# A decoder block: the head's transfers and casts in another order, and four background steps moved from Down to Up

## The chip, the cores and the metric

The kernel runs on one core of a Trainium2 chip. The metric is the device time of one execution in microseconds. A core has the engines TensorE (PE in the profile, with its weight loads as PEld), VectorE (DVE), ScalarE (ACT), GpSimd (POOL) and SyncE (SP); a DMA is issued by an instruction on the queue of one of them (here nearly always SP) and carried out by 16 DMA engines.

## The reference

One layer of a pre-norm decoder block in float32, 2048 tokens of width 1024:

```python
h = rmsnorm(x, norm_mix_g)
u = einsum('bsd,dc->bsc', h, w_in)                  # 1024 x 3584
gate_b, gate_c, v, x_r, g = split(u, ...)
y_conv = gate_b * causal_dwconv(gate_c * v, conv_w)
xr     = causal_dwconv(x_r, rnn_conv_w) + rnn_conv_b
y_rnn  = rg_lru(xr, w_a, b_a, w_x, b_x, lam) * gelu(g)
y = concat([rmsnorm(y_conv, g_norm_conv), rmsnorm(y_rnn, g_norm_rnn)])
x = x + einsum('bsc,cd->bsd', y, w_out)             # 1536 x 1024
z = square(relu(einsum('bsd,df->bsf', rmsnorm(x, norm_mlp_g), w_mlp_in)))   # 1024 x 4096
x = x + einsum('bsf,fd->bsd', z, w_mlp_out)         # 4096 x 1024
out = rmsnorm(x, final_norm_g)
```

`rg_lru` is a gated linear recurrence along the sequence: two block-diagonal projections, sigmoids, an exponential and a scan.

## The kernel before

**Numbers.** Every float32 operand of a matmul is split into a high part (a cast to fp32r, on ACT) and a low part (the difference, on VectorE); a product is the sum of three matmul passes: high by high, low by high and high by low. `split_into` (L179 to 181) does the split for weights. So a weight tile goes through DMA ("raw" or "w"), ACT ("w_hi") and DVE ("w_lo") before TensorE can use all of it.

**Stages.** The tokens are cut into four blocks of 512. Blocks 0 and 1 run through plain mixers (input projection by columns, conv, recurrence, output projection by rows, named "po"), blocks 2 and 3 through paired ones. The MLP takes two blocks at a time and has two halves, Up (w_mlp_in, "up", L854) and Down (w_mlp_out, "dn", L972), both with the seven products of a Strassen-Winograd scheme, in the order 1, 2, 6, 5, 7, 3, 4. Up walks 8 column slices of 7 products; Down 4 slices (s = 0 to 3) of 7 products of two halves (i is the product, a the half), some 5.44 us each. n counts products (Up) or halves (Down). `BG_FROM` (L40), the loop over Up and the loop over Down (around L2203) decide at which n a background step is taken.

**Background work.** The paired mixers need sums of weight tiles. They are made ahead of time by a generator: `prepare_sums` (63 steps) and `prepare_out_sums` (21 steps, L1283 to 1320; tiles w_out and t, three groups of seven steps). A step has up to two VectorE rows, a cast on ACT and DMAs to and from DRAM. `step()` is called in the mixer of block 1 (18 calls), in Up (30 calls) and in Down (37 calls) of the first MLP pair.

**The head.** Before the first product, x (transposed, in quarters "xT", two transfers of 256 KB each) and the first column unit of w_in (in quarters "raw", 256 KB) are loaded (L354 to 365). Quarters 0 and 1 of w are issued on ACT's queue, 2 and 3 on SP's, behind their xT. TensorE meanwhile runs warm-up matmuls on ones (L485, L487). For each quarter ACT scales xT to h_hi (L494) and casts w_hi (L498), VectorE makes h_lo (L499) and w_lo (L508), and TensorE runs 12 matmuls "start_x" (L515). After four quarters follows the next unit, "start_g" (L239). A small activation on `warm` (L369 to 370) loads the table of Sqrt ahead of time. In `lru_take`, the last three columns of the token block before ("halo") are copied into the first columns of xr_in, on ACT (L632); the new halo is saved on GpSimd (L637).

**What sets the order.** The program is written engine-agnostic in source order and laid out by a scheduling framework, which keeps the source order of an engine only in regions marked for manual scheduling. These are: the head (ACT, DVE and PE), the pair before the MLP (PE, ACT and DVE) and the MLP (PE). The mixers of blocks 0 and 1 are laid out by the scheduler, ACT and DVE of the MLP as well.

Of the kernel before, what the change touches and what calls it, by code (L numbers as in the profile page):

```python
# [9 lines left out]
F32 = mybir.dt.float32  # L10
F32R = mybir.dt.float32r
AF = mybir.ActivationFunctionType
ALU = mybir.AluOpType
MUL, ADD, SUB, MAX = ALU.mult, ALU.add, ALU.subtract, ALU.max

P = 128
# [20 lines left out]
IN_AHEAD = 3  # L37
SOONER = 200
PERIOD = 4
BG_FROM = 14  # L40
BG_UNITS = 24
BG_STEPS = 2
ORDER = (1, 2, 6, 5, 7, 3, 4)
# [21 lines left out]
def block_kernel(  # L65
# [15 lines left out]
    nc = tc.nc  # L81
    V = nc.vector
# [7 lines left out]
    cp = ctx.enter_context(tc.tile_pool(name="cp", bufs=1))  # L90
# [15 lines left out]
    def temp(name, shape=(P, 2, TB), dt=F32):  # L106
        if name in elsewhere:
            return wp.tile(list(shape), dt, tag="w", name=name)
        return tp.tile(list(shape), dt, tag="t", name=name)

    def wtile(name, shape, dt=F32):
        return wp.tile(list(shape), dt, tag="w", name=name)
# [25 lines left out]
    units = []  # L138
# [11 lines left out]
    raws = {}  # L150
# [125 lines left out]
    make_identity(nc, ident)  # L276
    ones_raw = temp("ones_raw", (P, P))
    nc.gpsimd.memset(ones_raw, 1.0)
    ones_r = cp.tile([P, P], F32R, name="ones_r")
    nc.scalar.copy(ones_r, ones_raw)  # L280
    ones = ones_r.bitcast(F32)
# [65 lines left out]
    def start_w(u, i):  # L347
        srcs, shape = units[u][1]
        raws.setdefault(u, []).extend(load_tiles(srcs[i : i + 1], shape, "raw", wtile))
# [2 lines left out]
    prm = cp.tile([P, nrows], F32, name="prm")  # L352
    nc.sync.dma_start(prm, rows_t)
    for q in range(4):  # L354
        r = temp("xT")
        for i in range(2):
            k0 = 256 * q + 128 * i
            nc.sync.dma_start(r[:, i, :], x_t[k0 : k0 + P, 0:TB])
        xtt[0, q] = r
        if q % 2 == 0:  # L360
            raws.setdefault(0, []).append(wtile("raw", units[0][1][1]))
        ks = slice(2 * (q % 2), 2 * (q % 2) + 2)
        (nc.scalar if q < 2 else nc.sync).dma_start(
            raws[0][q // 2][:, ks, :], units[0][1][0][q // 2][:, ks, :]
        )
    start_w(1, 0)
    start_w(1, 1)
    load_x(0)
    warm = cp.tile([P, 1], F32, name="warm")  # L369
    nc.scalar.activation(warm, ones_raw[:, 0:1], AF.Sqrt)  # L370
    off = {}
    o = 0
    for nm, n in ROWS:
# [86 lines left out]
    def new_h():  # L460
        return (
            hp.tile([P, KD, TB], F32R, tag="h", name="h_hi"),
            hp.tile([P, KD, TB], F32R, tag="h", name="h_lo"),
        )
# [15 lines left out]
    with tc.manual_schedule(  # L480
        engines={nc.scalar.engine, nc.vector.engine, nc.tensor.engine}
    ):
        h = new_h()
        for _ in range(WARM):
            nc.tensor.matmul(start_x[:, 0, :P], ones_raw, ones_raw, start=True, stop=True)  # L485
        for _ in range(WARM):
            nc.tensor.matmul(start_x[:, 0, :P], ones_raw, ones_raw, start=True, stop=True)  # L487
        his = [wtile("w_hi", units[0][1][1], F32R) for _ in range(2)]
        los = [wtile("w_lo", units[0][1][1], F32R) for _ in range(2)]
        w = (his, los)  # L490
        for q in range(4):
            n, ks = q // 2, slice(2 * (q % 2), 2 * (q % 2) + 2)
            for k in (2 * q, 2 * q + 1):
                nc.scalar.activation(  # L494
                    h[0][:, k], xtt[0, q][:, k % 2], AF.Copy, scale=gmix[:, k : k + 1]
                )
                if k % 2 == 0:
                    nc.scalar.copy(his[n][:, ks], raws[0][n][:, ks])  # L498
                V.scalar_tensor_tensor(  # L499
                    h[1][:, k],  # L500
                    xtt[0, q][:, k % 2],
                    gmix[:, k : k + 1],
                    h[0][:, k].bitcast(F32),
                    MUL,
                    SUB,
                )
                if k % 2 == 0:
                    V.tensor_tensor(  # L508
                        los[n][:, ks], raws[0][n][:, ks], his[n][:, ks].bitcast(F32), SUB
                    )  # L510
        for q in range(4):
            for n, (a, c) in enumerate(((0, 0), (0, 1), (1, 0))):
                for k in (2 * q, 2 * q + 1):
                    for j in range(2):
                        nc.tensor.matmul(  # L515
                            start_x[:, j],
                            w[a][k // 4][:, k % 4, j * P : (j + 1) * P],
                            h[c][:, k],
                            start=k == 0 and n == 0,
                            stop=k == KD - 1 and n == 2,  # L520
                        )
        raws.pop(0)
        cursor[0] = 1
        split_unit(1)
        w = take("g0", ahead=0)
        load_unit(2)
        s2 = squares(0, range(NT))
        split_unit(2)
        diag = diagonal(norm_rows(s2, NT), NT)
        start_g = psum("start_g")  # L530
        mm_cols(start_g, w, h, 0, ks=range(4))
        mm_cols(start_g, w, h, 1, ks=range(4))
        mm_cols(start_g, w, h, 0, ks=range(4, KD))
        mm_cols(start_g, w, h, 1, ks=range(4, KD))
        w = take("x1", ahead=0)
        start_x1 = psum("start_x1")
        mm_cols(start_x1, w, h, 0, ks=range(4))
        mm_cols(start_x1, w, h, 1, ks=range(4))
        bc = spread(diag, NT)
        mm_cols(start_x1, w, h, 0, ks=range(4, KD))  # L540
        mm_cols(start_x1, w, h, 1, ks=range(4, KD))
        nc.scalar.copy(row0[:, 0], bc)
        nc.scalar.activation(row0[:, 1], bc, AF.Square)
# [39 lines left out]
    halo = cp.tile([P, NLRU, 3], F32, name="halo")  # L583
# [45 lines left out]
    def lru_take(pr, psx, row=None):  # L629
        c0 = 2 * pr  # L630
        xr_in = wide("xr_in", 3)
        nc.scalar.copy(xr_in[:, :, 0:3], halo[:, c0 : c0 + 2, :])  # L632
        if row is None:
            nc.scalar.copy(xr_in[:, :, 3:], psx)
        else:
            V.tensor_mul(xr_in[:, :, 3:], psx, row)
        nc.gpsimd.tensor_copy(halo[:, c0 : c0 + 2, :], xr_in[:, :, TB : TB + 3])  # L637
        return xr_in
# [1189 lines left out]
    def pair_before_mlp(b, ups):  # L1828
# [172 lines left out]
        xs = {}  # L2001
        ss = {}
        gm = cp.tile([P, KD], F32, name="gm")
        nc.sync.dma_start(gm, mlp_g_t)

        def square(b, t, i, first):
            if first:
# [105 lines left out]
    def mlp(b, ups, r0, r1, t2, rest, xs, turns_at, prepared):  # L2113
# [6 lines left out]
        for n in range(-LEAD1, len(seq)):  # L2120
# [12 lines left out]
            s, i = seq[n]  # L2133
# [11 lines left out]
            later_operands(n, r0, r1, t2)  # L2145
            if b < PAIRED and BG_FROM <= n < len(seq) - 6 and i != 3:
                step()
# [22 lines left out]
        more = b + 2 < NB  # L2170
        seq = [(s, i, a) for s in range(NS // 2) for i in ORDER for a in range(2)]
        fetched = 5
        for n in range(-LEAD2, len(seq)):
            m = n + LEAD2
            if m < len(seq):
                s, i, a = seq[m]
# [12 lines left out]
            while fetched < min(n + LEAD2 + 3, len(seq)):  # L2189
                s, i, a = seq[fetched]  # L2190
                downs[s].fetch(i, a, Z)
                fetched += 1
            s, i, a = seq[n]
# [6 lines left out]
                downs[s].multiply_last(ends[1].tiles(ends[0]))  # L2200
            if i == 7 and s + 1 < NS // 2:
                downs[s + 1].load(a)
            if more and n > 6 and (s < 2 or s == 2 and i != 4 or i in (1, 2)):  # L2203
                step()
            if more and s == NS // 2 - 1:
                if (i, a) == (6, 1):
# [2 lines left out]
                if i in (7, 3):  # L2209
                    q = 2 * (i == 3) + a  # L2210
# [123 lines left out]
```

## Time and profile before

| what | value |
|---|---|
| median of 3 runs (lowest to highest) | 2114.38 us (2113.29 to 2116.30) |
| the profiled execution | 2114.52 us |
| its span, first to last instruction | 2112.7 us |
| mean granted TensorE clock | 0.998 |
| busy ScalarE / VectorE | 52% / 76% |

The profile shows one execution. Its page gives the busy time of the engines, the costliest groups of instructions and the chain that ended last; the trace behind it gives a timeline (start, duration, engine, line, operation, output <- inputs, and in brackets the idle time before it with what ended it), waits by engine, and tables by stretch of time. The chain that ended last is TensorE for 85% of the span:

```profile
PE 85%; DVE 4%; issue 1%; DMA 1%; ACT 1%; SPq 0%; DVEq 0%; ACTq 0%
DMA  9988889743576779778765656776343455854432
```

The second row is the busy share of the DMA engines in 40 slices of 52.8 us; the first six slices, up to 317 us, have 8 or 9 tenths.

### The profile page before, as it was taken

Reading aid. Unit: us, or ns where it says so; the run is one execution under the profiler, and the core shown is the slowest. Engines: PE = TensorE matmul, PEld = TensorE weight load, DVE = VectorE, ACT = ScalarE, POOL = GpSimd, SP = SyncE. Lnnn points to the kernel's source line nnn. Section 1 sums busy time; section 2 is a strip of 40 time slices with the busy share of each in tenths; the row PEclk is TensorE's granted clock in tenths of the full one; section 3 lists DMA queues with packets and bytes.
Section 4 is the critical chain, followed back from the end, with each engine's and each line's share of the span. In section 5 each row is a group of like instructions: output and inputs, shape, how many; then the busy total and the mean of one; then the engine's idle time right before and its main releaser. Section 6 shows DMA issues by size and latency. Waiting matters only on the chain.

```text
span 2112.7 us, 25180 instructions
## 1 busy us (share of the span) xinstructions
PE 2098.0 (99%) x9396; PEld 1727.0 (82%) x9396; DVE 1603.8 (76%) x1857; ACT 1106.0 (52%) x1448; POOL 52.2 (2%) x62
## 2 busy tenths in 40 slices
PE   9999999999999999999999999999999999999998
PEld 7888888888888888888788887888888888888886
DVE  6889637858766688998997876785886765887776
ACT  6885357626554554444456888234764333333344
POOL 0000001000000000000100100000000000000000
PEclk9999999999999999999999999999999999999999
DMA  9988889743576779778765656776343455854432
GB/s 323 331 313 321 316 333 338 296 170 114 186 269 250 278 265 336 271 268 303 288 228 206 223 210 220 271 264 212 120 164 135 149 180 209 306 182 149 140 120 80
DMA packets 204875, 492.99 MB, mean 233 GB/s; under 512 B 15952, under 2 KB 80464, under 8 KB 204752
## 3 DMA queue, kind: packets, MB, share of 16 engines
q1 hardware_dynamic: 202768, 486.13, 64.0%
q10 hardware_dynamic: 1984, 5.24, 0.6%
q8 instruction: 74, 1.21, 0.2%
q14 instruction: 49, 0.40, 0.1%
HBM read 324.59 MB, written 166.72 MB: 233 GB/s over the span
## 4 chain that ended last, share of the span: by engine, by line
PE 85%; DVE 4%; issue 1%; DMA 1%; ACT 1%; SPq 0%; DVEq 0%; ACTq 0%
PE up L854 40%; PE dn L972 26%; PE po L266 5%; PE wo_x L1798 3%; PE ps_g L239 2%; PE ps_x L239 2%; PE wo_w L1798 2%; PE ps_c L239 1%; PE ps_v L239 1%; PE wo_y L1798 1%; PE tps L1652 1%; PE dn L991 1%; PE psri L1411 1%; PE ps_b L239 1%; DVE u L759 0%
## 5 line engine op out<-in xcount | busy, mean ns | idle before, releaser
L854 PE MATMUL up<-H,w_hi 128*128 128x512 f32 x2576 | 794.9, 390 | 0.0
L854 PEld LDWEIGHTS up<-H,w_hi 128*128 128x128 f32 x2576 | 482.4, 188 | 102.6 <-issue 1.8
L854 PE MATMUL up<-H,w_lo 128*128 128x512 f32 x1288 | 501.4, 389 | 0.0
L972 PE MATMUL dn<-w_lo,z_hi 128*128 128x512 f32 x864 | 336.5, 389 | 1.2 <-DVE w_lo L181 1.2
L972 PE MATMUL dn<-w_hi,z_lo 128*128 128x512 f32 x864 | 336.1, 389 | 0.0
L972 PE MATMUL dn<-w_hi,z_hi 128*128 128x512 f32 x864 | 336.1, 389 | 0.0
L854 PEld LDWEIGHTS up<-H,w_lo 128*128 128x128 f32 x1288 | 241.8, 188 | 51.0 <-DVE w_lo L181 0.7
L180 ACT CAST z_hi<-z 128x1024 fp32r<-128x1024 f32 x112 | 118.0, 1053 | 272.3 <-PE dn L972 214.9
L181 DVE TENSOR_TENSOR w_lo<-w,w_hi 128x1024 fp32r<-128x1024 f32 x156 | 190.2, 1221 | 75.4 <-ACT w_hi L180 27.5
L180 ACT CAST w_hi<-w 128x1024 fp32r<-128x1024 f32 x156 | 162.8, 1049 | 138.8 <-PE up L854 67.9
L972 PEld LDWEIGHTS dn<-w_lo,z_hi 128*128 128x128 f32 x864 | 162.2, 188 | 35.7 <-DVE w_lo L181 2.3
L972 PEld LDWEIGHTS dn<-w_hi,z_lo 128*128 128x128 f32 x864 | 162.2, 188 | 33.8
L972 PEld LDWEIGHTS dn<-w_hi,z_hi 128*128 128x128 f32 x864 | 162.2, 188 | 33.7
L1004 DVE TENSOR_TENSOR x<-dn,x 128x1024 f32<-128x1024 f32 x108 | 130.6, 1220 | 23.9 <-PE dn L972 23.7
L181 DVE TENSOR_TENSOR z_lo<-z,z_hi 128x1024 fp32r<-128x1024 f32 x112 | 136.5, 1218 | 5.4 <-ACT z_hi L180 5.4
L866 ACT COPY snap<-up 128x1024 f32<-128x1024 f32 x48 | 48.7, 1014 | 67.6 <-PE up L854 67.3
L871 ACT ACTIVATE snap<-snap 128x1024 f32<-128x1024 f32 x33 | 35.1, 1062 | 74.4 <-DVE snap L891 28.5
L181 DVE TENSOR_TENSOR w_lo<-raw,w_hi 128x1024 fp32r<-128x1024 f32 x44 | 53.3, 1220 | 13.2 <-ACT w_hi L180 10.7
L266 PE MATMUL po<-w_hi,y_hi 128*128 128x512 f32 x192 | 60.0, 394 | 0.4 <-DVE ys_B L623 0.4
L266 PE MATMUL po<-w_hi,y_lo 128*128 128x512 f32 x192 | 59.7, 391 | 0.3 <-DVE y_lo L596 0.3
L1798 PE MATMUL wo_x<-w_o,y_hi 128*128 128x512 f32 x192 | 59.8, 392 | 0.0
L266 PE MATMUL po<-w_lo,y_hi 128*128 128x512 f32 x192 | 59.3, 389 | 0.0
(415 smaller groups left out, 3290.3 us busy)
## 6 DMA issues: line engine op xcount, KB each, us to landing
z<-d_z SPq DMA_DIRECT2D x112, 512.0 KB, 6.2
w<-in_w_mlp_in_dram SPq DMA_DIRECT2D x64, 512.0 KB, 6.1
d_z<-snap SPq DMA_DIRECT2D x64, 512.0 KB, 3.5
w_hi<-d_w SPq DMA_DIRECT2D x55, 512.0 KB, 6.6
w_lo<-d_w SPq DMA_DIRECT2D x55, 512.0 KB, 6.2
d_z<-z SPq DMA_DIRECT2D x48, 512.0 KB, 3.4
w<-in_w_mlp_out_dram SPq DMA_DIRECT2D x48, 512.0 KB, 7.5
d_w<-w_hi SPq DMA_DIRECT2D x40, 512.0 KB, 6.2
```

Source lines behind the costliest of these rows:

```text
L180: nc.scalar.copy(hi, src)
L181: return (lo_engine or V).tensor_tensor(lo, src, hi.bitcast(F32), SUB).ins
L239: nc.tensor.matmul(ps[:, j, lo:hi], ws[k // 4][:, k % 4, j * P : (j + 1) * P], hs[:, k, lo:hi], start=k == 0 and i == 0, stop=k == KD - 1 ...
L266: nc.tensor.matmul(ps[:, half, :], ys[:, j, t * P : (t + 1) * P], ws[j][:, 0, half * 512 : (half + 1) * 512], start=first and i == 0, stop ...
L854: nc.tensor.matmul(ps[:, j, :], ws[:, k, j * P : (j + 1) * P], hs(k), start=i in (1, 2, 5) and k == 0 and n == 0, stop=k == 3 and n == len ...
L866: made_at["snap"] = nc.scalar.copy(t, ps).ins
L871: nc.scalar.activation(t, t, AF.Relu)
L972: nc.tensor.matmul(ps[t // 2][:, t % 2, :], zs[:, p, t * P : (t + 1) * P], ws[:, p, :], start=i in (1, 2, 5) and a == 0 and p == 0 and n == 0,
L991: nc.tensor.matmul(self.x[t // 2][:, t % 2, :], zs[:, p, t * P : (t + 1) * P], ws[:, p, :], start=False, stop=a == 1 and p == 1 and n == 2 ...
L1004: V.tensor_add(xt[b, th, dh], ps[th], xt[b, th, dh])
L1411: nc.tensor.matmul(ps[:, e, :], ws[own, c - gates[2], :], xsrc[own, j, :], start=i == 0, stop=i == 2,)
L1798: nc.tensor.matmul(ps[t // 2][:, t % 2, :], ys[:, j, t * P : (t + 1) * P], ws[:, j, :], start=first and n == 1, stop=final and n == 6 * le ...
```

## The change

1. `BG_FROM` goes from 14 to 10, and Down takes no background steps in s = 3 any longer (products 1 and 2, both halves). Up makes 34 calls and Down 33, so every step that comes after n = 9 is taken four calls sooner.
2. The warm Sqrt activation is issued before the cast of ones_r. Both used a table load of their own; the program now has one there.
3. In the head w's quarter 0 is issued on ACT's queue, and quarters 1 to 3 on SP's, each ahead of the xT quarter of the same number.
4. In each quarter w_hi is cast before both h_hi, and w_lo is made after both h_lo.
5. The copy of halo into xr_in goes from ACT to GpSimd, and the load of gm from SP's queue to GpSimd's.

```diff
--- before.py
+++ after.py
@@ -37,7 +37,7 @@
 IN_AHEAD = 3
 SOONER = 200
 PERIOD = 4
-BG_FROM = 14
+BG_FROM = 10
 BG_UNITS = 24
 BG_STEPS = 2
 ORDER = (1, 2, 6, 5, 7, 3, 4)
@@ -276,6 +276,8 @@
     make_identity(nc, ident)
     ones_raw = temp("ones_raw", (P, P))
     nc.gpsimd.memset(ones_raw, 1.0)
+    warm = cp.tile([P, 1], F32, name="warm")
+    nc.scalar.activation(warm, ones_raw[:, 0:1], AF.Sqrt)
     ones_r = cp.tile([P, P], F32R, name="ones_r")
     nc.scalar.copy(ones_r, ones_raw)
     ones = ones_r.bitcast(F32)
@@ -352,22 +354,20 @@
     prm = cp.tile([P, nrows], F32, name="prm")
     nc.sync.dma_start(prm, rows_t)
     for q in range(4):
+        if q % 2 == 0:
+            raws.setdefault(0, []).append(wtile("raw", units[0][1][1]))
+        ks = slice(2 * (q % 2), 2 * (q % 2) + 2)
+        (nc.sync if q else nc.scalar).dma_start(
+            raws[0][q // 2][:, ks, :], units[0][1][0][q // 2][:, ks, :]
+        )
         r = temp("xT")
         for i in range(2):
             k0 = 256 * q + 128 * i
             nc.sync.dma_start(r[:, i, :], x_t[k0 : k0 + P, 0:TB])
         xtt[0, q] = r
-        if q % 2 == 0:
-            raws.setdefault(0, []).append(wtile("raw", units[0][1][1]))
-        ks = slice(2 * (q % 2), 2 * (q % 2) + 2)
-        (nc.scalar if q < 2 else nc.sync).dma_start(
-            raws[0][q // 2][:, ks, :], units[0][1][0][q // 2][:, ks, :]
-        )
     start_w(1, 0)
     start_w(1, 1)
     load_x(0)
-    warm = cp.tile([P, 1], F32, name="warm")
-    nc.scalar.activation(warm, ones_raw[:, 0:1], AF.Sqrt)
     off = {}
     o = 0
     for nm, n in ROWS:
@@ -490,12 +490,11 @@
         w = (his, los)
         for q in range(4):
             n, ks = q // 2, slice(2 * (q % 2), 2 * (q % 2) + 2)
+            nc.scalar.copy(his[n][:, ks], raws[0][n][:, ks])
             for k in (2 * q, 2 * q + 1):
                 nc.scalar.activation(
                     h[0][:, k], xtt[0, q][:, k % 2], AF.Copy, scale=gmix[:, k : k + 1]
                 )
-                if k % 2 == 0:
-                    nc.scalar.copy(his[n][:, ks], raws[0][n][:, ks])
                 V.scalar_tensor_tensor(
                     h[1][:, k],
                     xtt[0, q][:, k % 2],
@@ -504,10 +503,9 @@
                     MUL,
                     SUB,
                 )
-                if k % 2 == 0:
-                    V.tensor_tensor(
-                        los[n][:, ks], raws[0][n][:, ks], his[n][:, ks].bitcast(F32), SUB
-                    )
+            V.tensor_tensor(
+                los[n][:, ks], raws[0][n][:, ks], his[n][:, ks].bitcast(F32), SUB
+            )
         for q in range(4):
             for n, (a, c) in enumerate(((0, 0), (0, 1), (1, 0))):
                 for k in (2 * q, 2 * q + 1):
@@ -629,7 +627,7 @@
     def lru_take(pr, psx, row=None):
         c0 = 2 * pr
         xr_in = wide("xr_in", 3)
-        nc.scalar.copy(xr_in[:, :, 0:3], halo[:, c0 : c0 + 2, :])
+        nc.gpsimd.tensor_copy(xr_in[:, :, 0:3], halo[:, c0 : c0 + 2, :])
         if row is None:
             nc.scalar.copy(xr_in[:, :, 3:], psx)
         else:
@@ -2001,7 +1999,7 @@
         xs = {}
         ss = {}
         gm = cp.tile([P, KD], F32, name="gm")
-        nc.sync.dma_start(gm, mlp_g_t)
+        nc.gpsimd.dma_start(gm, mlp_g_t)
 
         def square(b, t, i, first):
             if first:
@@ -2200,7 +2198,7 @@
                 downs[s].multiply_last(ends[1].tiles(ends[0]))
             if i == 7 and s + 1 < NS // 2:
                 downs[s + 1].load(a)
-            if more and n > 6 and (s < 2 or s == 2 and i != 4 or i in (1, 2)):
+            if more and n > 6 and (s < 2 or s == 2 and i != 4):
                 step()
             if more and s == NS // 2 - 1:
                 if (i, a) == (6, 1):
```

Lines of the changed kernel after the head are two below those of the kernel before. Since a scheduler lays out much of the program, an edit can move rows far away from it. Three places follow.

ACT from the start of the program (the head). Before:

```order
L363 DMA raw<-in_w_in_dram 128x2x256
L280 ACT_TABLE_LOAD
L280 CAST ones_r<-ones_raw 128x128
L363 DMA raw<-in_w_in_dram 128x2x256
L370 ACT_TABLE_LOAD
L370 ACTIVATE warm<-ones_raw 128x1
L494 ACTIVATE h_hi<-xT,prm 128x512
L632 COPY xr_in<-halo 128x2x3 x3
L498 CAST w_hi<-raw 128x512
L494 ACTIVATE h_hi<-xT,prm 128x512 x2
L498 CAST w_hi<-raw 128x512
```

and in the changed kernel:

```order
L360 DMA raw<-in_w_in_dram 128x2x256
L280 ACT_TABLE_LOAD
L280 ACTIVATE warm<-ones_raw 128x1
L282 CAST ones_r<-ones_raw 128x128
L493 CAST w_hi<-raw 128x512
L495 ACTIVATE h_hi<-xT,prm 128x512 x2
L493 CAST w_hi<-raw 128x512
L495 ACTIVATE h_hi<-xT,prm 128x512 x2
L493 CAST w_hi<-raw 128x512
L495 ACTIVATE h_hi<-xT,prm 128x512 x2
```

One of two table loads is gone from ahead of the first h_hi, the issue of the second quarter of w and the copies of halo are gone, and each w_hi stands in front of both h_hi of its quarter.

DVE in the output projection of block 0, in the rows that lead to the last y_lo of the recurrence (v<-r,v is the decay of the recurrence, w_lo_1389, w_lo_1472 and w_lo_1476 are low parts of coming weights, y_lo_1375 and y_lo_1462 of the projection's operand). Before:

```order
L738 TENSOR_TENSOR gc_1312<-ps_c_1263,row0_125 128x1024
L181 TENSOR_TENSOR w_lo_1389<-raw_1245,w_hi_1388 128x1024
L605 TENSOR_TENSOR v_573<-v_573,v_1142 128x1024
L700 TENSOR_TENSOR gi_1315<-gi_1315,xr_1147 128x1024
L430 TENSOR_SCALAR diag_hi_1356<-ident_81,rs_x_1034 128x128 x2
L431 SCALAR_TENSOR_TENSOR diag_lo_1357<-ident_81,rs_x_1034,diag_hi_1356 128x128 x2
L430 TENSOR_SCALAR diag_hi_1356<-ident_81,rs_x_1034 128x128 x2
L431 SCALAR_TENSOR_TENSOR diag_lo_1357<-ident_81,rs_x_1034,diag_hi_1356 128x128 x2
L181 TENSOR_TENSOR w_lo_1472<-raw_1380,w_hi_1471 128x1024
L714 SCALAR_TENSOR_TENSOR v_1339<-r_1314,v_1339 128x1024
L181 TENSOR_TENSOR w_lo_1476<-raw_1382,w_hi_1475 128x1024
L715 TENSOR_SCALAR r_1314<-v_1339 128x1024
```

and in the changed kernel:

```order
L712 SCALAR_TENSOR_TENSOR v_1339<-r_1314,v_1339 128x1024
L181 TENSOR_TENSOR w_lo_1389<-raw_1245,w_hi_1388 128x1024
L713 TENSOR_SCALAR r_1314<-v_1339 128x1024
L594 SCALAR_TENSOR_TENSOR y_lo_1375<-s_448,prm_92,y_hi_1374 128x512
L714 SCALAR_TENSOR_TENSOR v_1339<-v_1339 128x1024
L594 SCALAR_TENSOR_TENSOR y_lo_1375<-s_448,prm_92,y_hi_1374 128x512
L744 TENSOR_TENSOR cv_1449<-ps_v_1400,gc_1312 128x2x512
L755 TENSOR_SCALAR u_1453<-cv_1449,prm_92 128x512 x2
L716 TENSOR_TENSOR gi_1315<-gi_1315,v_1339 128x1024
L181 TENSOR_TENSOR w_lo_1472<-raw_1380,w_hi_1471 128x1024
L719 SCALAR_TENSOR_TENSOR v_1339<-r_1314,state_398,gi_1315 128x512
L181 TENSOR_TENSOR w_lo_1476<-raw_1382,w_hi_1475 128x1024
```

w_lo_1389 and w_lo_1472 stood ahead of v<-r,v, and stand behind it now; w_lo_1476 stood right behind it, and stands five rows later. The w_hi casts that these need moved on ACT in the same way.

DVE in the last slice of Down (s = 3). x<-dn,x adds a product of Down to its sum, L1304 to L1308 and w_out<-w_out,sum_hi are background rows, and w_lo<-w_7852 before is w_lo<-w_7871 in the changed kernel. Before:

```order
L1004 TENSOR_TENSOR x_6365<-dn,x_6365 128x1024
L181 TENSOR_TENSOR z_lo<-z,z_hi 128x1024
L181 TENSOR_TENSOR w_lo<-w_7302,w_hi 128x1024
L1304 TENSOR_TENSOR t_7948<-w_out 128x1024
L1305 TENSOR_TENSOR w_out<-w_out 128x1024
L942 TENSOR_TENSOR t_8001<-w_7858,w_7856 128x1024
L1308 TENSOR_TENSOR w_out<-w_out 128x1024
L181 TENSOR_TENSOR t_7948<-t_7948,sum_hi 128x1024
L181 TENSOR_TENSOR z_lo<-z,z_hi 128x1024
L181 TENSOR_TENSOR w_lo<-w_7852,w_hi 128x1024
```

and in the changed kernel:

```order
L181 TENSOR_TENSOR w_lo<-w_7318,w_hi 128x1024
L181 TENSOR_TENSOR w_out<-w_out,sum_hi 128x1024
L1002 TENSOR_TENSOR x_6384<-dn,x_6384 128x1024
L1002 TENSOR_TENSOR x_6386<-dn,x_6386 128x1024
L181 TENSOR_TENSOR w_out<-w_out,sum_hi 128x1024
L181 TENSOR_TENSOR z_lo<-z,z_hi 128x1024
L181 TENSOR_TENSOR w_lo<-w_7871,w_hi 128x1024
L940 TENSOR_TENSOR t_8027<-w_7877,w_7875 128x1024
L1002 TENSOR_TENSOR x_6697<-dn,x_6697 128x1024
L941 TENSOR_TENSOR w_7875<-w_7875,w_7871 128x1024
```

Between w_lo<-w_7302 (w_lo<-w_7318 now) and the next w_lo stood four background rows and a sum of weights; now there are two background rows, and the sum comes behind it.

## The prediction

> **What bounds the kernel now.** The page's first part comes first: TensorE is busy almost throughout, so a change that leaves its matmuls alone can win only what is missing from that line.
>
> ```profile
> PE 2098.0 (99%) x9396; PEld 1727.0 (82%) x9396; DVE 1603.8 (76%) x1857; ACT 1106.0 (52%) x1448; POOL 52.2 (2%) x62
> ```
>
> The span is 2112.7 us and the profiled execution's own time 2114.52, so 1.82 us lie outside the span; the median of the runs shown, 2114.38, is 0.14 below that execution. Of the span, 2112.7 - 2098.0 = 14.7 us have no matmul in them. The view of waits, cut to TensorE, says where it stood still (us in total, times, longest), and it has five rows only:
>
> ```profile
> PE start_x L515 <- ACT w_hi L498: 2.4, 1, 2.4
> PE dn L972 <- DVE w_lo L181: 1.2, 2, 0.6
> PE start_x L485 <- POOL ones_raw L278: 1.1, 1, 1.1
> PE po L266 <- DVE ys_B L623: 0.4, 1, 0.4
> PE po L266 <- DVE y_lo L596: 0.3, 1, 0.3
> ```
>
> The head, two waits in Down and the output projection of blocks 0 and 1 are the places to look at; the tail (some 9 us behind the last matmul) is not touched. Then the timeline of the head, with each row's start and duration:
>
> ```profile
> 1.23 1.28 ACT L280 ACT_TABLE_LOAD   x1 [1.23 <-PEq L2300]
> 2.82 1.28 ACT L370 ACT_TABLE_LOAD   x1
> 3.85 1.58 PE L487 MATMUL start_x<-ones_raw 128*128 128x128 f32 x12
> 6.24 0.72 ACT L494 ACTIVATE h_hi<-xT,prm 128x512 fp32r<-128x512 f32 x1 [1.92 <-DMA xT<-in_x_t_dram]
> 6.87 0.38 ACT L632 COPY xr_in<-halo 128x6 f32<-128x6 f32 x3
> 7.15 0.61 ACT L498 CAST w_hi<-raw 128x512 fp32r<-128x512 f32 x1
> 7.82 2.07 PE L515 MATMUL start_x<-h_hi,w_hi 128*128 128x512 f32 x4 [2.38 <-ACT w_hi L498]
> 12.07 1.08 PE L515 MATMUL start_x<-h_hi,w_hi 128*128 128x512 f32 x4
> 14.80 1.07 PE L515 MATMUL start_x<-h_hi,w_hi 128*128 128x512 f32 x4
> 20.24 0.39 PE L239 MATMUL start_g<-h_hi,w_hi 128*128 128x512 f32 x1
> ```
>
> The warm-up matmuls end at 3.85 + 1.58 = 5.43, and TensorE waits for the chain "xT lands, h_hi, halo copies, w_hi". From the second quarter on, a quarter of 12 matmuls takes 14.80 - 12.07 = 2.73 us, 0.227 each. The first took 12.07 - 7.82 = 4.25. The table by stage says why (PEclk is the last number but two):
>
> ```profile
> 5.00:6.00 1.00, 0.43 (x4) 0.24 (x3) 0.00 (x0) 0.00 (x0) 0.00 (x0) 1.00 1.01 338
> 6.00:7.00 1.00, 0.00 (x0) 0.00 (x0) 0.00 (x1) 0.76 (x3) 0.00 (x0) 1.00 1.00 374
> 8.00:9.00 1.00, 1.00 (x3) 0.78 (x4) 1.00 (x2) 1.00 (x3) 0.00 (x0) 0.50 1.04 333
> 11.00:12.00 1.00, 1.00 (x6) 0.83 (x5) 1.00 (x3) 1.00 (x2) 0.00 (x0) 1.00 1.02 341
> ```
>
> The granted clock was halved at 8 us and back at 11, right behind the idle stretch; so the head lost 2.4 us of waiting and some 1.5 more to the clock. The DMA share is 1.0 there: transfers land one behind the other, 262 KB at about 374 GB/s, which is 0.70 us each.
>
> **Head: what it gains.** The order of ACT's instructions in the changed kernel is: one table load (1.28 us, at 1.23), the warm activation, ones_r, then the first w_hi cast, then both h_hi. ACT is so free by about 3.1 instead of 4.3, and w_hi is out of the way as soon as w's first quarter is in; that quarter has ACT's queue to itself. After xT lands only h_hi (0.72) stands before the first matmul; in the rows above it was 7.82 - 6.24 = 1.58, so 0.86 us come from the order. The rest comes from the landing. Before, w's second quarter shared the engines from the first microseconds; now its 0.70 us of traffic stand behind xT's first two transfers. I take xT's first half at 5.5 instead of 6.2 and the first matmul at 6.25. TensorE then idles 6.25 - 5.43 = 0.8 us instead of 2.4. In the first quarter the second h_hi follows a landing 0.7 later, and w_lo now stands behind both h_lo, which together cost about 0.35 us on the path; I set 3.07 us for the quarter, and 3 x 2.73 for the other three. start_g begins at 6.25 + 3.07 + 8.19 = 17.5 instead of 20.24: **-2.8 us**, on the assumption that the clock stays full. If it is halved again for the same stretch, the first quarter costs some 1.5 us more and the gain is 1.3. The upper bound is 3.2 (no small wait in the first quarter).
>
> The lead has to be fed. start_g's third matmul needs the next unit's w_lo, and that chain is bound by a landing:
>
> ```profile
> 15.27 1.05 ACT L180 CAST w_hi<-raw 128x1024 fp32r<-128x1024 f32 x1 [0.94 <-DMA raw<-in_w_in_dram]
> 16.36 1.23 DVE L181 TENSOR_TENSOR w_lo<-raw,w_hi 128x1024 fp32r<-128x1024 f32 x1 [1.24 <-ACT w_hi L180]
> ```
>
> The bytes ahead of it are the same, so it is ready at 16.36 + 1.23 = 17.59 again, and needed at 17.5 + 0.45 = 17.95: just in time. A larger lead would not be kept. The gm transfer leaves SP's queue (it stood behind x, the warm-up's last load) and three small copies leave ACT; GpSimd is 2% busy, and its nearest row is a copy of the same kind:
>
> ```profile
> 165.59 1.11 POOL L747 COPY haloc<-cv 128x4 f32<-128x4 f32 x1 [16.32 <-DVE cv L746]
> ```
>
> A halo copy there lies beside the product whose conv it feeds (10.9 us for one of 48 matmuls), so both are at nothing, from -0.4 (the row at 6.87, if ACT were short) to +1.1 for a conv that waits once.
>
> [...]
>
> **Down: what it gains.** The two waits of 0.6 us are in the last of the four column slices (s = 3), where VectorE runs back to back and background work stands between an accumulation and the w_lo that TensorE needs next:
>
> ```profile
> 996.72 1.22 DVE L1004 TENSOR_TENSOR x<-dn,x 128x1024 f32<-128x1024 f32 x1 [1.50 <-PE dn L972]
> 1000.13 1.22 DVE L1304 TENSOR_TENSOR t<-w_out 128x1024 f32<-128x1024 f32 x1
> 1007.07 1.22 DVE L181 TENSOR_TENSOR w_lo<-w,w_hi 128x1024 fp32r<-128x1024 f32 x1
> 1007.40 0.39 PE L972 MATMUL dn<-w_hi,z_hi 128*128 128x512 f32 x1
> 1008.34 0.50 PE L972 MATMUL dn<-w_lo,z_hi 128*128 128x512 f32 x1 [0.55 <-DVE w_lo L181]
> 1030.05 0.39 PE L972 MATMUL dn<-w_hi,z_hi 128*128 128x512 f32 x1
> 1031.04 0.50 PE L972 MATMUL dn<-w_lo,z_hi 128*128 128x512 f32 x1 [0.60 <-DVE w_lo L181]
> ```
>
> Starts are 0.227 apart elsewhere, so the two cost 1008.34 - 1007.40 - 0.23 = 0.71 and 1031.04 - 1030.05 - 0.23 = 0.76. VectorE issues one such row every 1.15 us (996.72 to 1007.07 is nine steps). From the x addition to the first late w_lo there are ten rows, four of them background (two are quoted); in the changed order there are five. The second late w_lo has two background rows ahead of it, which are gone too. Five and two rows are 5.7 and 2.3 us of slack against 0.7 and 0.8 of waiting. So **-1.47 us**, bounds 0 and -1.5.
>
> The steps do not vanish: each comes four calls earlier. Four run in Up at n = 10 to 13, and the third block of out sums now lies on the turn from s = 1 to s = 2. I counted VectorE's rows there: from the addition behind n = 27 to the w_lo of n = 32 there are 17 rows of 1.15 us, 19.6 us, ready some 1.0 to 1.3 us before TensorE comes to it. No stall, but little margin, a rival. In Up, TensorE waits for nothing, and a step is at most two VectorE rows and a cast beside products of 10.9 us each; at nothing, bounds 0 and the 0.7 of one such stall.
>
> **Output projection of block 0: a loss.** Here nothing was edited, but the scheduler lays the rows out anew. On ACT three w_hi casts move from in front of the sigmoids to behind them, and the w_lo that belong to them move with them, to a place where VectorE is never idle.
>
> ```profile
> 148.41 0.69 ACT L694 ACTIVATE r<-psri,prm 64x512 f32<-64x512 f32 x1
> 161.43 1.22 DVE L714 SCALAR_TENSOR_TENSOR v<-r,v 128x1024 f32<-128x1024 f32 x1 [0.76 <-ACT r L708]
> 179.50 0.75 DVE L596 SCALAR_TENSOR_TENSOR y_lo<-s,prm,y_hi 128x512 fp32r<-128x512 f32 x1
> 180.31 0.74 PE L266 MATMUL po<-w_hi,y_lo 128*128 128x512 f32 x2 [0.30 <-DVE y_lo L596]
> ```
>
> From 161.43 to 179.50 VectorE runs without a gap, and the second half of y_lo is already 0.6 us late (0.30 shown as idle, 0.57 against the usual spacing). Counted in both orders from "v<-r,v" to that y_lo, the change has two w_lo more, 2 x 1.15 = 2.3 us; the start of the stretch stays: ahead of "r" on ACT one w_hi cast is gone (1.05), its input s comes one VectorE row sooner (1.15), and a table load (1.28) and the first sigmoid (0.69) now stand behind s instead of ahead of it, which is 0.2 us sooner in all. TensorE's own order is the same, so the stall grows from 0.6 to some 2.6: **+2.0 us**, bounds 0 (the chain starts that much earlier) and +2.5.
>
> **Output projection of block 1: a small gain.** In the new order one y_hi and one y_lo fewer stand before bcs and ys_B:
>
> ```profile
> 420.33 0.97 PEld L615 LDWEIGHTS po<-ones_r,v 128*128 128x128 f32 x8 [0.58 <-ACT bcs L1135]
> 423.03 0.73 PE L266 MATMUL po<-w_hi,y_hi 128*128 128x512 f32 x2 [0.40 <-DVE ys_B L623]
> ```
>
> The two waits cost about 0.31 and 0.56 us against the usual spacing; a y_hi half is 0.7 us on ACT, a y_lo half 0.7 on VectorE, so most of both goes: **-0.7 us**, bounds 0 and -0.87.
>
> **Sum:** 2114.52 - 2.8 + 2.0 - 0.7 - 1.47 = 2111.55 for an execution like the profiled one, and 0.14 less, 2111.4, against the median.
>
> **Rivals.**
> 1. *The re-laid order costs nothing in the output projection.* For it: the loss rests on a count of rows, and the chain of block 0 hangs on several engines, each of which could start sooner. Against it: y_lo was late already and nothing ahead of it went away. Then 2111.4 - 2.0 = 2109.4.
> 2. *The half clock stays.* For it: 0.50 was granted right after an idle stretch in which TensorE had worked before and after. Against it: only a third of the idle time is left. Or the landing does not move, as the engines carry 338 to 374 GB/s already, which costs 0.7. Either gives 2111.4 + 1.5 = 2112.9, at most.
> 3. *The stall in Down only moves.* The turn from s = 1 to s = 2 has about 1 us of margin; two more VectorE rows (2.3 us) there, and it waits 1.2 us, as s = 3 does now: 2111.4 + 1.5 = 2112.9.
> 4. *Slower.* The four early steps take tiles of the common pool while Up still holds the norm's and the sums' tiles. If one takes a tile that a load of Up's weights needs, that load is issued a product later and TensorE waits for the whole chain behind it:
>
> ```profile
> L180 ACT CAST w_hi<-w 128x1024 fp32r<-128x1024 f32 x156 | 162.8, 1049 | 138.8 <-PE up L854 67.9
> L181 DVE TENSOR_TENSOR w_lo<-w,w_hi 128x1024 fp32r<-128x1024 f32 x156 | 190.2, 1221 | 75.4 <-ACT w_hi L180 27.5
> w<-in_w_mlp_in_dram SPq DMA_DIRECT2D x64, 512.0 KB, 6.1
> ```
>
>  That is 6.1 + 1.05 + 1.22 = 8.4 us, 2111.4 + 8.4 = 2119.8. It decides from the point where the pool has no free tile at n = 12 or 13. Against it: loads go out three products ahead (33 us), and no wait of TensorE in Up is in the view above.
>
> **How the numbers follow.** Chances: the forecast 0.40, rival 1 0.30, rival 2 0.12, rival 3 0.07, rival 4 0.11. 0.2% of 2114.38 is 4.2 us, about what a measurement of this kernel can tell from no change: faster is below 2110.15, slower above 2118.6. Rival 1 is faster in nine cases of ten (0.27), the forecast in its better fifth (0.09): 0.36. Slower is nearly all of rival 4: 0.10. The rest, 0.54, is within 0.2%. The range's lower end takes every term at its better bound, 2114.4 - 3.2 - 0.87 - 1.5 = 2108.8; the upper takes the poorest head and the full loss in the projection, with the gain of Down and half of that in block 1: 2114.4 - 1.3 + 2.5 - 1.47 - 0.4 = 2113.7, with 1.2 for a stall that moves, 2114.9. Of the same, the forecast's own spread is 2110.2 to 2112.6.
>
> **What would show it.** Right: the first data matmul near 6.3 and start_g near 17.5, no clock of 0.5 between 7 and 11 us, no wait of dn for w_lo in s = 3, one wait of po for y_lo of about 2.5 us near 177, and waits of po for bcs and ys_B gone or halved. Wrong: a first quarter still at 4 us (rival 2), no long y_lo wait (rival 1), a dn wait near 950 (rival 3), a wait of up for w_hi or w_lo in the first 14 products (rival 4). A matmul count or order that differs outside the places named, or waits of several us in the first 150 us, would make the sum itself wrong.

## The result and the profile after

| | before | changed |
|---|---|---|
| median of 19 runs each (lowest to highest) | 2114.55 us (2112.84 to 2117.75) | 2117.75 us (2116.18 to 2120.26) |
| ratio, 95% interval | | 1.0016 [1.0009, 1.0023] |
| profiled execution, span | 2114.52, 2112.7 us | 2118.50, 2116.7 us |
| mean granted clock | 0.998 | 0.996 |

The change makes the kernel 3.2 us slower; the forecast was 3.0 us faster (2111.4), with 2114.9 as the upper end of its range. The view of TensorE's waits in the changed kernel (us in total, times, longest):

```profile
PE po L266 <- DVE y_lo L594: 4.9, 2, 3.6
PE start_x L485 <- POOL ones_raw L278: 1.1, 1, 1.1
PE dn L970 <- DVE w_lo L181: 0.8, 1, 0.8
PE start_x L513 <- ACT h_hi L495: 0.6, 1, 0.6
```

The head's wait fell from 2.4 to 0.6 us, Down's two waits in s = 3 and block 1's ys_B are gone. In their place stands one line that was 0.3 us before: po waiting for y_lo, now 4.9. (The dn wait of 0.8 lies in the second MLP, at 1830 us; it was 0 to 0.5 us in the executions of the experiments and is not followed here.)

The head in the changed kernel's timeline (start, duration):

```profile
4.79 0.72 ACT L495 ACTIVATE h_hi<-xT,prm 128x512 fp32r<-128x512 f32 x1 [0.29 <-DMA xT<-in_x_t_dram]
5.57 0.73 PE L513 MATMUL start_x<-h_hi,w_hi 128*128 128x512 f32 x2
6.89 0.73 PE L513 MATMUL start_x<-h_hi,w_hi 128*128 128x512 f32 x2 [0.59 <-ACT h_hi L495]
17.55 0.39 PE L239 MATMUL start_g<-h_hi,w_hi 128*128 128x512 f32 x1
```

start_g begins at 17.55 instead of 20.24, 2.7 us sooner. Then the output projection of block 0, TensorE's rows and VectorE's:

```profile
175.38 0.61 PE L266 MATMUL po<-w_lo,y_hi 128*128 128x512 f32 x2
179.59 1.22 PE L266 MATMUL po<-w_hi,y_lo 128*128 128x512 f32 x2 [3.60 <-DVE y_lo L594]
183.79 1.22 PE L266 MATMUL po<-w_hi,y_lo 128*128 128x512 f32 x2 [1.27 <-DVE y_lo L594]
...
162.51 1.23 DVE L712 SCALAR_TENSOR_TENSOR v<-r,v 128x1024 f32<-128x1024 f32 x1 [1.02 <-ACT r L706]
178.80 0.74 DVE L594 SCALAR_TENSOR_TENSOR y_lo<-s,prm,y_hi 128x512 fp32r<-128x512 f32 x1
183.00 0.74 DVE L594 SCALAR_TENSOR_TENSOR y_lo<-s,prm,y_hi 128x512 fp32r<-128x512 f32 x1
```

Both halves of y_lo are late. The second one starts 3.5 us later than before (183.00 against 179.50), for a TensorE that is 2.7 us earlier. And the pair of matmuls behind each wait takes 1.22 us, where it took 0.74 before (the row at 180.31), because of the clock (last number but two):

```profile
178.00:180.00 2.00, 0.41 (x1) 0.41 (x2) 2.00 (x4) 1.31 (x2) 0.00 (x0) 0.70 0.93 330
184.00:185.00 1.00, 1.00 (x3) 0.81 (x4) 1.00 (x2) 0.10 (x1) 0.00 (x0) 0.50 1.02 418
187.00:188.00 1.00, 1.00 (x4) 0.81 (x3) 1.00 (x2) 1.00 (x2) 0.07 (x1) 0.50 0.00 0
189.00:190.00 1.00, 1.00 (x6) 0.77 (x5) 1.00 (x2) 0.00 (x0) 0.00 (x0) 0.99 0.00 0
```

A mean of 0.70 from 178 to 180 puts the fall at 178.8; the clock is back at 189.0. VectorE, by contrast, has no gap from 162.51 to 190.

The ledger, by the start of the same TensorE row in both executions: -2.6 us behind the head, +5.85 behind the waits for y_lo (so this place costs 8.5), +4.8 behind block 1's projection (a gain of 1.1, of which 0.9 lie in that projection's rows), +3.1 behind Down's s = 3 (a gain of 1.7), +4.0 at the end (the wait at 1830). The profiled execution is 0.75 us above the median. Of the 8.5 us, 6.1 have come together at the second late pair: it starts at 183.79 instead of 180.31, 3.5 us later, on a TensorE that had been 2.6 ahead. It starts when VectorE has made its y_lo, so the half clock between the two waits costs nothing of its own. The other 2.4 are the twelve matmuls behind that start, some 0.43 us each instead of 0.23.

### The profile page after: what moved, and what is told of

Same layout as the page of the kernel before. It is cut to its first block, busy times and chain, and to the rows that moved or that the text cites. A ratio compares the mean times of both kernels' runs of the same rounds, so it can differ in the third digit from the quotient of the medians.

```text
span 2116.7 us, 25169 instructions
## 1 busy us (share of the span) xinstructions
PE 2100.1 (99%) x9396; PEld 1728.8 (82%) x9396; DVE 1604.1 (76%) x1857; ACT 1104.9 (52%) x1439; POOL 56.8 (3%) x71
## 4 chain that ended last, share of the span: by engine, by line
PE 93%; DVE 4%; ACT 1%; issue 1%; DMA 1%; SPq 0%; POOL 0%; DVEq 0%; ACTq 0%; POOLq 0%
PE up L852 40%; PE dn L970 26%; PE po L266 6%; PE ps_g L239 3%; PE wo_x L1796 3%; PE ps_x L239 3%; PE ps_v L239 2%; PE wo_w L1796 2%; PE ps_c L239 2%; PE ps_b L239 2%; PE wo_y L1796 1%; PE tps L1650 1%; PE dn L989 1%; PE psri L1409 1%; PE start_x L239 1%
```

## Experiments: what delays y_lo

Three theories were put against each other. A: part 4, the cast order in the head, makes the scheduler lay out ACT and VectorE anew for the first 200 us, and that layout is late. B: TensorE's lead alone is too large for a VectorE chain that cannot follow. C: the halo copies on GpSimd delay the recurrence. The layouts themselves speak for A as far as they can: with the head's casts in the old order and the rest of the change kept, the rows of VectorE behind the head stand in the order of before up to block 0's end, and with the casts alone nearly all stand in the order of the changed kernel.

**The casts back.**

```diff
-            nc.scalar.copy(his[n][:, ks], raws[0][n][:, ks])
             for k in (2 * q, 2 * q + 1):
...
+                if k % 2 == 0:
+                    nc.scalar.copy(his[n][:, ks], raws[0][n][:, ks])
...
```

> The changed kernel with the head's casts in the old order (h_hi, w_hi, h_hi; w_lo behind the first h_lo); everything else of the change is kept. Theory A (the cast order makes the scheduler lay out the mixers anew, and that layout delays y_lo in the output projection of block 0): start_g near 18, the two waits of po for y_lo (3.6 and 1.3 us in the changed kernel) shrink to at most 2.5 us together, no clock of 0.5 near 180 us, time 2110.5 to 2113. Theory B (TensorE's lead alone runs into a VectorE chain that cannot follow): waits of 4 us or more and the half clock stay, time 2115.5 to 2118. Theory C (halo copies on GpSimd delay the recurrence): as the changed kernel, 2117 to 2119.

Measured: 2111.43 us, 0.9988 [0.9980, 0.9997] of before. start_g at 17.84. Its waits of TensorE:

```profile
PE start_x L485 <- POOL ones_raw L278: 1.1, 1, 1.1
PE po L266 <- DVE y_lo L596: 1.1, 1, 1.1
PE dn L972 <- DVE w_lo L181: 0.5, 1, 0.5
PE po L266 <- DVE ys_B L623: 0.4, 1, 0.4
```

One wait of 1.1 us for y_lo, and the clock 1.00 throughout from 176 to 190. With nearly the whole lead (2.4 us) the long wait is gone: against B.

**The casts alone,** in the kernel before (the same lines, the other way round).

> The kernel before with only the head's cast order of the change. Theory A: the new layout comes with it, so po waits for y_lo 3 us or more near 180 and the clock may fall to 0.5 behind it, with Down's two waits still there: 2116 to 2121, in spite of a head that is up to 1 us shorter. Theory B: TensorE has little lead here, so no wait above 1 us at that place: 2113 to 2114.5. Theory C: halo copies are on ACT here, so no wait either: 2113 to 2114.5.

Measured: 2119.59 us, 1.0025 [1.0015, 1.0034]. The two rows of TensorE at the place:

```profile
180.25 1.22 PE L266 MATMUL po<-w_hi,y_lo 128*128 128x512 f32 x2 [3.37 <-DVE y_lo L594]
184.45 1.22 PE L266 MATMUL po<-w_hi,y_lo 128*128 128x512 f32 x2 [1.27 <-DVE y_lo L594]
```

Two moved statements, no halo copy on GpSimd, a lead of only 1.8 us (start_g at 18.47), and the same two waits and the half clock (0.50 from 179.0 to 189.2 us, by the means of its stretches). A holds; B and C fall as causes by themselves.

**The halo copies back on ACT** (`nc.scalar.copy` in `lru_take`).

> The changed kernel with the halo copies back on ACT. Theories A and B: as the changed kernel, 2116.5 to 2119, with the waits of po for y_lo of 4 to 6 us in sum. Theory C: the waits shrink by half or more, 2111 to 2114.

Measured: 2118.66 us, 1.0021 [1.0013, 1.0030]; waits for y_lo 5.1 us in two. Against C once more.

**The background steps back** (BG_FROM 14, and Down's condition of before).

> The changed kernel with the background steps as before (Up from n = 14, Down in s = 3 too). If moving the four steps is worth what Down's two waits cost, and nothing in Up: both waits of dn for w_lo (0.6 us each) are back and the time is 1.5 us longer than the changed kernel's, 2118.5 to 2120. If the early steps cost time in Up or on the turn of Down's slices: 2117.5 or less. The waits near 180 us are the same as in the changed kernel by all theories.

Measured: 2119.05 us, 1.0022 [1.0013, 1.0032]. Down's waits are back (1.4 us in three), and the waits for y_lo are 5.8 us. The step to the changed kernel is 1.3 us by these medians, near the 1.5 expected, though the two intervals overlap.

### What in the new layout is late

The stretch ahead shows it. The busy time of VectorE (third of the numbers with a count) from 50 to 60 us, and the sum from 50 to 160, in the kernel before and then in the changed one:

```profile
50.00:60.00 10.00, 10.00 (x50) 7.76 (x49) 8.45 (x22) 7.39 (x10) 0.00 (x0) 1.00 1.01 347
sum 110.00, PE 110.00 PEld 89.00 DVE 91.40 ACT 90.87 POOL 6.64; mean PE 10.00 PEld 8.09 DVE 8.31 ACT 8.26 POOL 0.60
```

```profile
50.00:60.00 10.00, 10.00 (x49) 7.74 (x49) 4.42 (x18) 7.22 (x14) 0.00 (x0) 1.00 1.05 396
sum 110.00, PE 110.00 PEld 88.96 DVE 86.74 ACT 85.75 POOL 17.93; mean PE 10.00 PEld 8.09 DVE 7.89 ACT 7.80 POOL 1.63
```

In this stretch VectorE has done 4.7 us less work; it had entered it 1.8 us ahead, as far as its rows at 50 us show, so 2.9 are missing in all by 160. Two w_lo that were done by then (1.15 each) are still to do, where it has no gap. The first that moved is the weight unit v0. Its w_hi and w_lo before, and below in the changed kernel, with what stood on ACT at their old place:

```profile
52.57 2.06 ACT L180 CAST w_hi<-raw 128x1024 fp32r<-128x1024 f32 x2
55.82 1.23 DVE L181 TENSOR_TENSOR w_lo<-raw,w_hi 128x1024 fp32r<-128x1024 f32 x1
```

```profile
52.20 0.68 ACT L692 ACTIVATE r<-psri,prm 64x512 f32<-64x512 f32 x1
55.59 0.63 ACT L1125 ACTIVATE xq<-xq 128x512 f32<-128x512 f32 x1 [2.71 <-DMA xq<-in_x_dram]
67.09 1.04 ACT L180 CAST w_hi<-raw 128x1024 fp32r<-128x1024 f32 x1
70.52 1.22 DVE L181 TENSOR_TENSOR w_lo<-raw,w_hi 128x1024 fp32r<-128x1024 f32 x1
```

The casts of v0 fell behind a row that waits for a transfer, so ACT stood still for 2.7 us in which it had cast them before. Both w_lo went from an idle stretch of VectorE to a busy one, and each later unit's w_lo queued up behind. Until then the chain of the recurrence had kept TensorE's lead and more: the row xr at 58.28 before is at 54.28 in the changed kernel. At 125 us the chain is 1.2 us later than before. So s, which ACT needs at 150 us, comes no sooner, though one w_lo fewer stands ahead of it (before, then changed):

```profile
149.15 1.22 DVE L728 TENSOR_TENSOR s<-v,s 128x1024 f32<-128x1024 f32 x1
149.19 1.22 DVE L726 TENSOR_TENSOR s<-v,s 128x1024 f32<-128x1024 f32 x1
```

To see whether this one unit is the cause, the whole change was run with its split given priority in the scheduler:

```diff
-            if v < len(units) and units[v][0] == "oB1":
+            if v < len(units) and (units[v][0] == "oB1" or v == 6):
                 with tc.high_priority(SOONER):
                     split_unit(v, lo_engine)
```

> The changed kernel, whole, but the split of one weight unit (v0, sixth behind x0: two w_hi casts on ACT, two w_lo on VectorE) is given the scheduler's high priority, as oB1 has it. In the changed kernel this split runs 15 us later than before, and every later w_lo of block 0 behind it. Theory A (that late split is where the new layout loses its time): the w_lo of block 0 stand where they stood before, start_g stays near 17.5, po waits for y_lo at most 1.5 us, full clock near 180, 2110.5 to 2112.5. Rival (the head's larger lead, or the cast order in the head as such): waits of 3.5 us or more, 2115.5 to 2118.5.

Measured: 2110.51 us, 0.9985 [0.9976, 0.9994]. The waits:

```profile
PE start_x L485 <- POOL ones_raw L278: 1.1, 1, 1.1
PE start_x L513 <- ACT h_hi L495: 1.0, 1, 1.0
PE po L266 <- DVE ys_B L621: 0.4, 1, 0.4
PE po L266 <- DVE y_lo L594: 0.3, 1, 0.3
```

VectorE is busy 91.3 of the 110 us from 50 to 160, 4.6 more than in the changed kernel, "v<-r,v" starts at 159.33 instead of 162.51, and y_lo costs 0.3 us of waiting. All of the cast order is kept (start_g at 18.11, its wait for h_hi 1.0 us in this execution). So the long wait is not the head's doing as such: it comes with the late splits, which the head's order set off in the scheduler and one unit's priority takes back. The priority moves more than v0: of VectorE's 192 rows of before between 22 and 190 us, 189 stand in the order of before again, against 145 in the changed kernel. What v0's split alone would cost, with all other rows kept, is not shown.

### Can TensorE work around it

**The y_hi passes of three token tiles first, then y_lo,** in the unit oB1 of block 0.

```diff
...
+                if pr == 1 and b == 0:
+                    if t == 2:
+                        for only in ((0, 1), (2,)):
+                            for n in range(3):
+                                for j in range(2):
+                                    mm_rows(po[n], y, w, j, n, False, False, only)
+                    continue
```

> The changed kernel with its new layout kept; only the order of TensorE's passes in the second unit of block 0's output projection (oB1) is another: the 24 matmuls with y_hi of all three token tiles first, then the 12 with y_lo. Theory: TensorE has 24 x 0.227 = 5.4 us of work before it needs the first y_lo instead of 0.9, so the waits for y_lo fall from 4.9 us to 1.5 or less, no half clock, 2109.5 to 2113. Rival (VectorE and ACT bound the whole projection, and TensorE meets the next unit's y_hi as much too early): a new wait of 3 us or more at the next unit, 2115 or more.

Measured: 2117.22 us, 1.0010 [1.0002, 1.0019]: the rival's time, though the waits are not at the next unit's y_hi. The rows of TensorE that wait:

```profile
183.87 2.57 PE L268 MATMUL po<-w_hi,y_lo 128*128 128x512 f32 x10 [2.47 <-DVE y_lo L596]
189.35 1.54 PE L615 MATMUL po<-ones_r,v 128*128 128x1 f32 x8 [1.51 <-ACT bcs L1135]
```

TensorE was busy until 181.4 and then met the second half of y_lo and, after it, a row that hangs on the same chain. The theory counted the work ahead of the first y_lo, but the second half comes 4.2 us after it, and both halves are needed one behind the other now. The clock is halved here too, 0.50 from 189.8 to 196.6 us by the means of its stretches. With VectorE late by several us, another order on TensorE moves the wait.

**Zeros in the wait.**

```diff
...
+            for n in range(fill if i == 2 else 0):
+                nc.tensor.matmul(ps[:, n % 2, :P], zeros, zeros, start=False, stop=False)
...
```

> The changed kernel with 16 and 12 matmuls of zeros (128x128, adding nothing) on TensorE in front of the two products that wait for y_lo, about 3.4 and 2.6 us. The y_lo come no sooner. Theory (the idle TensorE has its clock halved, and the matmuls behind the wait pay for it): granted clock 1.0 from 176 to 190 us, the second wait ends near 183.8 as before, and the matmuls behind it run at 0.227 instead of 0.427: 2 to 3 us less than the changed kernel, 2114.5 to 2116. Rival (the half clock costs nothing, since VectorE's chain bounds the products behind it too): 2117 to 2119.

Measured: 2117.76 us, 1.0017 [1.0008, 1.0026]: no gain in the time, as the rival said. The profile says something else of the place itself:

```profile
178.00:180.00 2.00, 2.00 (x21) 2.00 (x19) 2.00 (x4) 1.20 (x2) 0.00 (x0) 1.00 0.99 335
184.00:186.00 2.00, 2.00 (x12) 1.67 (x11) 2.00 (x3) 1.22 (x2) 0.00 (x0) 1.00 1.03 422
```

The clock stays at 1.00, and the first row behind the projection, sps, starts 2.25 us sooner than in the changed kernel (second row):

```profile
218.66 0.95 PE L617 MATMUL sps<-ones_r,cv 128*128 128x1 f32 x8
220.91 0.95 PE L613 MATMUL sps<-ones_r,cv 128*128 128x1 f32 x8
```

That is within the 2 to 3 us that were expected, though this execution had entered with 0.6 us less lead, and near the 2.4 of the ledger. About 1 us of it is then lost again in block 1, where waits for bcs and ys_B come back, and the span ends only 0.7 us shorter. The rest to the equal medians stays open.

**v0 ahead and the passes together.**

> The two edits together: v0 with high priority and the y_hi passes first. If both work as said, TensorE waits for nothing in block 0's output projection and keeps the head's 2.7 us and Down's 1.5: 2109.5 to 2111, faster than the kernel before by more than 3 us. If one of them only moves the wait on: 2111.5 to 2114.

Measured: 2110.65 us, 0.9983 [0.9974, 0.9992]: the same as v0 ahead alone. The wait for y_lo is gone and that for ys_B is 1.2 us instead of 0.4.

### What the parts of the change are worth

These three go from the version with v0 ahead (2110.51 us), where the layout is nearly the same in all.

**The head's transfers in the old order.** (The loop of before, with w's quarters behind their xT.)

> The changed kernel with v0 ahead (2110.5 us), and the head's transfers in the old order (w's quarters 0 and 1 on ACT's queue, 2 and 3 behind their xT). Theory (the transfer order carries the head's gain): xT's first half lands 0.7 us or more later, TensorE idles 1.5 us or more ahead of the first product, start_g at 19 or later, 2111.8 to 2113. Rival (the single table load and the cast order carry it): start_g before 18.5, 2110 to 2111.3.

Measured: 2111.59 us, 0.9988 [0.9979, 0.9997]; start_g at 19.00, 0.9 us later, and the first data matmul at 6.80 instead of 5.76. The time lies between what the theory (2111.8 or more) and the rival (2111.3 or less) expected, and the two intervals overlap. xT's first half is awaited longer (1.45 us instead of 0.29 in the changed kernel):

```profile
6.03 0.72 ACT L495 ACTIVATE h_hi<-xT,prm 128x512 fp32r<-128x512 f32 x1 [1.45 <-DMA xT<-in_x_t_dram]
```

**Two table loads again** (the warm activation behind ones_r).

> The changed kernel with v0 ahead, and the warm activation back behind the cast of ones_r, so that ACT loads two tables (2.6 us, to 4.3 us). Theory: w_hi begins at 4.3 instead of 3.9, still ahead of xT's landing near 4.8 to 5.0, so the first product starts at most 0.4 us later: 2110.2 to 2111.2. Rival: the load's whole 1.3 us reach the path: 2111.5 to 2112.5.

Measured: 2110.94 us, 0.9983 [0.9974, 0.9992]; start_g at 18.31. ACT's first cast starts at 4.24 instead of 3.9, and h_hi then waits for nothing but that cast; the difference of 0.4 us is within the intervals.

**The background steps as before.**

> The changed kernel with v0 ahead, and the background steps as before. Theory: the two waits of dn for w_lo (0.5 to 0.6 us idle, 0.7 with the slower restart each) are back at the last slice of Down, 2111.5 to 2112.5. Rival (the early steps cost in Up what they save in Down): 2110 to 2111.

Measured: 2112.92 us, 0.9991 [0.9982, 1.0000], 2.4 us slower than v0 ahead and 0.4 above what was expected. The waits of Down are back:

```profile
PE dn L970 <- DVE w_lo L181: 1.2, 2, 0.6
```

The span of this execution is 1.7 us longer than that of the one with v0 ahead (2110.2 against 2108.5 us); the rest of the 2.4 is within what the two intervals leave open.

## Why the prediction was wrong

- **The head, forecast -2.8, came out near in sum, by luck in its parts:** start_g at 17.55 against 17.5 (2.74 us sooner, booked as 2.8). Rival 2 (the half clock stays) did not come: 1.00 from 5 us on. But two misses cancel. The first data matmul starts at 5.57 and not 6.25, since the first h_hi can start at 4.79 and not 5.5. The first quarter takes 3.75 us and not 3.07, since the second h_hi starts 1.33 us behind the first (6.12), where a landing 0.7 later was assumed. In the other executions with the same head start_g lies between 17.6 and 18.2, a gain of 2.0 to 2.7. The split into causes was wrong too: the order of casts was given 0.86 us, but the version without it starts start_g at 17.84, in the range of the others, and in the kernel before the casts alone bring 1.8 (18.47). The parts do not add up, since neither of these versions shows the half clock at its head: from 8.5 us on their matmuls start 0.23 us apart, where the first four of before, from 7.82, start 0.47 apart. The half clock at the head of before, some 1.5 us, goes with either part. The transfers give 0.9 beside v0 ahead, the single table load some 0.2 to 0.4, each from one execution and near the scatter or within it.
- **Down, forecast -1.47, was right:** 1.7 in the ledger, a little over its bound of 1.5, and the waits come back when the steps do, in two versions. Neither Up nor the turn from s = 1 to s = 2 shows a wait, so rivals 3 and 4 did not come.
- **Block 1's projection, forecast -0.7:** -0.9 in its own rows, right in kind and at its bound of 0.87.
- **Block 0's projection, forecast +2.0 with +2.5 as its bound, is the step that failed:** +8.5. Its place and direction were right; three parts of its sum were not. First, "the start of the stretch stays" was worked out from three rows on ACT just ahead of it, as 0.2 us sooner. It was 1.1 us later (162.51 against 161.43). The count on ACT held: from v<-s to "v<-r,v" the changed kernel takes 1.0 us more, and the table load and the sigmoid less the cast are 0.9. What failed is the input s, booked as 1.15 us sooner: it comes at 149.19 against 149.15, since the splits that began to slip at v0's, 100 us upstream, had made VectorE's chain 1.0 us late by then. Second, the sum took the head's lead as a gain and the projection's wait as a separate term. The lead belongs in that wait: TensorE came 2.7 us sooner to a chain that had lost its own lead. 1.1 later, 2.3 for the two w_lo (counted), and 2.7 of lead make 6.1 us at the second half of y_lo, where the sum had 2.0. Third, the clock fell behind these waits, which adds 2.4 us and makes 8.5; the prediction used this mechanism for the head and not here.
- The forecast asked only whether the rows at the place had moved, and of "waits of several us in the first 150 us" it said that they would make the sum wrong; there were none on TensorE, the loss ran along VectorE unseen by it. The range's upper end had no case for the lead and the layout together: rival 1 was that the loss might not come, none that it might be larger.

The time forecast, 2111.4, is what the change gives without its part 4 (2111.43), by chance: in that version block 0's projection costs 0.8 and not 2.0, and block 1's gains nothing. With part 4 and one line of priority it gives 2110.51, faster than both kernels (its interval lies below 1); a gain of 3.6 us over before by medians of the same session (2114.08).

## What to carry to other kernels

Where a scheduler lays out the program, compare the layouts of the whole program for each part of an edit by itself: here two statements in a head of 15 us moved the first weight split by 15 us and others along the next 100. Before a lead is booked as a gain, ask at each later place where TensorE only just waits whether its producer inherits the lead; add both shifts and then the clock. Where both traces are at hand, compare the busy time of the producing engine up to that place: VectorE had done 4.7 us less in the stretch ahead, in which TensorE did not wait at all.

## What the hardware showed that was not expected

The half clock does not follow a wait at once, nor each wait. Two rows each of the version with the halo copies back and of the one with the background steps back:

```profile
180.00:182.00 2.00, 0.99 (x2) 0.83 (x3) 2.00 (x3) 0.73 (x2) 0.00 (x0) 0.74 1.04 380
184.00:186.00 2.00, 0.79 (x3) 0.67 (x4) 2.00 (x3) 0.00 (x0) 0.00 (x0) 0.91 1.04 419
```

```profile
184.00:186.00 2.00, 1.94 (x6) 1.57 (x7) 2.00 (x2) 0.83 (x1) 0.00 (x0) 0.74 1.03 420
188.00:190.00 2.00, 2.00 (x9) 1.62 (x9) 2.00 (x4) 1.02 (x2) 1.06 (x1) 0.91 0.02 8
```

By the means, 0.50 holds from 181.0 to 184.4 in the first and from 185.0 to 188.4 in the second, 3.4 us each; in the changed kernel from 178.8 to 189.0, 10.2, which is three times that, and in the version with the y_hi passes first 6.8, twice that. In the kernel before, at the head, it holds from 7.4 to 10.8, 3.4 again. In the version with the background steps back, a wait of 3.3 us (TensorE idle from about 176.6) was followed by full clock, and the next of 2.55 by the half. So the same loss on VectorE (waits for y_lo of 4.9 us in the changed kernel, 5.1 and 5.8 in these two) costs a different number of microseconds in each execution. What tells these two waits apart is not shown: the longer one kept the full clock, and at the head of before a wait of 2.38 us went with the half clock.

Matmuls of zeros in the two waits (from 176.47 and from 181.43 us, until the products behind them start at 179.96 and 184.03) kept the clock at 1.00 from 174 to 196 us, so here it was enough that TensorE ran, though on zeros.
